# Moving the low parts of the first layer's weights to GpSimd, giving taps back to VectorE, and spreading reciprocals by transposes

## The chip, the cores and the metric

The kernel runs on one core of one Trainium2 chip. The metric is the device time of one execution in microseconds; the kernel before has a median of 1711.2 us over three runs. The engines are named as the profile names them: PE is TensorE (PEld its weight loads), DVE is VectorE, ACT is ScalarE, POOL is GpSimd, SP is SyncE, which issues the DMAs.

## The reference

Two layers over 1024 tokens of width 1024, in fp32. The first is a convolution module, the second an attention with three head groups. Each is followed by `x <- LayerNorm(alpha * x + sublayer(x))`.

```python
# layer 1
a, a_gate, z = split(x @ w_in + b_in, 3)                 # 1024 -> 3 x 1024
u = a * sigmoid(a_gate)
u = causal_depthwise_conv(u, w_dw, width=31) + b_dw       # 31 taps, each channel by itself
u = silu(layer_norm(u))                                   # over the channels
y = (u * silu(z)) @ w_out + b_out
# layer 2
k, v = x @ kv_w;  q, z = x @ w_in                         # 3 groups x 16 heads x 64
for each group (window, dilation) in (128, 1), (512, 4), (2048, 16):
    o, lse = banded_attention(q, k, v, alibi)
o = sum(softmax over the groups(lse) * o)
y = (o * silu(z)) @ w_out + b_out
```

## The kernel before

**Split precision.** Every large product is made of three products of fp32r operands: high part by high part, low by high, high by low. So each weight tile of 128x1024 is loaded (`raw`), its high part is made by a copy (`whi`, line 234 on ACT in the first layer, line 236 on POOL in the second), and its low part by a subtraction, `raw - hi` (`wlo`, line 243). The set `DVE_LO` says for which weights, counted in order of use, DVE does that subtraction; for the others POOL does it. Weights 0 to 23 are those of the input projection, 24 to 39 those of the out-projection, and from 40 on those of the second layer. The first two are made in four pieces. Each of `raw`, `whi` and `wlo` has two buffers.

**First layer.** Channels lie on the partitions, in eight blocks c = 0..7, and the tokens are in two halves h of 512. PE makes the value and the gate for the eight blocks (tiles `pa`, `pg`), then the eight blocks of z (`pz`). ACT and DVE make `u` from them. The convolution of block c is called `c<n>` for the first half and `d<n>` for the second. Of its 31 taps, tap 0 is on ACT; for the next `n_pool - 1` ACT makes a product (`cvt`, line 410) and POOL adds it (line 414); the rest are on DVE, multiply and add in one instruction, into a PSUM bank (`cva`, line 426). For the twelve convolutions of `MERGED` the two sums run side by side and DVE joins them at the end (line 438); the other four, `d4` to `d7`, continue POOL's sum on DVE. `stats` then makes the mean by a product with ones on PE (`mp`, line 451), the centred values (line 465), squares on ACT, their sums on POOL and PE (`vp`), a square root and a reciprocal; `apply` makes the normalised and gated values and splits them for the out-projection (`uh` on ACT, `ul` on DVE, line 537). The out-projection (`po`) follows for each half, then the post-norm, transposes of the result (`pt`, line 730) and the split `x1h`, `x1l`.

**Second layer.** For each of eight pairs of heads PE makes k, q (`pk`, `pq`), the gate (`pzb`) and v (`pv`), scores (`ps`), transposes of the weights of attention (`ptp`, line 1156) and the products with v (`av`). The attention of one pair is done in between the projections of the next. In `finish`, the reciprocals of the softmax sums, which stand with the tokens on the partitions, are widened by ACT to a tile `rx` of 64 equal columns for each head, and PE turns them, four blocks of 128x128 for each token half, by a product with the identity into a PSUM bank (`rb`, line 1302), which DVE multiplies into the output.

**Order.** The instructions are not written out by hand. Each step is added with its engine, an estimated cost, a priority, what it waits for, and buffers it takes and frees. `Order.run` plays a list schedule with these costs and latencies on simulated engines, and the program is then emitted in that order; so the costs set only the order of each engine's instructions and of the DMA issues, which stays fixed on the chip.

```python
        @on("pe", 0.88, (2.8, a.p, 5), [widen] + a.turned[1], take="cv", frees=[widen])
        def spread():
            q.t = bank("rb", "cv")
            for j in range(4):
                nc.tensor.matmul(q.t[:, j * P:(j + 1) * P], lhsT=q.x[:, j].rearrange("p i d -> p (i d)"), rhs=ident,
                                 start=True, stop=True)
```

Of the kernel before, what the change touches and what calls it, by code (L numbers as in the profile page):

```python
# [15 lines left out]
P = 128  # L16
D = 1024
T = 1024
KT = D // P
# [8 lines left out]
PAD = 32  # L28
N_POOL = dict.fromkeys(("d4", "d5", "d6", "d7"), 12)
PE_ORDER = "a0 a1 a2 a3 a4 a5 a6 a7 z0 z1 z2 z3 z4 z5 z6 z7".split()  # L30
DVE_ORDER = "c0d0 c1c2 d1c3 c4d2 c5c6 d3c7 s0 m0 d4d5 d6d7 s1 m1".split()
FIRST = 4
X_LATE = 0.6
DVE_LO = {0, 2, 3, 8, 9, 11, 12, 14, 15, 17, 19, 20, 23, 24, 25, 26, 27, 31, 33, 34, 35, 38, 39, 41, 42, 44, 45, 46, 90, 92, 93, 94, 98, 100, 101, 102, 103, 104, 105, 106, 108, 110, 111, 112, 113, 114, 115, 117, 118, 119, 124, 125, 126, 130, 131, 133, 134, 136}
PATHS = {(0, 1): 'dp', (1, 1): 'dd', (2, 1): 'pd', (3, 1): 'pd', (0, 0): 'pd', (2, 0): 'pd', (3, 0): 'dd'}
SUMS = [8, 4]
MERGED = "c0d0c1c2d1c3c4d2c5c6d3c7"
PAIRED = (1, 2, 3, 4)
RELEASE = 0.25
ENGINES = ("pe", "act", "dve", "pool", "dma", "none")  # L40
LATENCY = {(a, b): 2.0 if a == "dma" else 0.2 if a == "pe" else 0.27 if b == "pe" else 0.08 if a == "pool" else 0.15
# [8 lines left out]
class Step:  # L50
    def __init__(self, eng, cost, fn, prio, table, take):
        self.eng, self.cost, self.fn, self.prio, self.table, self.take = eng, cost, fn, prio, table, take
        self.waits, self.then, self.users, self.frees = 0, [], 0, []


class Order:
# [4 lines left out]

    def add(self, eng, cost, fn, prio, after=(), take=None, frees=(), table=None):
        step = Step(eng, cost, fn, prio, table, take)
        for o in after:
            step.waits += 1
            o.then.append(step)
        for o in frees:
            self.free(step, o)
        self.steps.append(step)
        return step  # L70
# [5 lines left out]
    def run(self):  # L76
# [8 lines left out]
        while True:  # L85
# [28 lines left out]
            while events and events[0][0] <= now:  # L114
                _, _, _, other, step = heapq.heappop(events)
                for o in step.frees if other is None else ():
                    o.users -= 1
                    if not o.users:
                        live[o.take] -= 1
                for o in step.then:  # L120
                    if o.eng == other:
                        o.waits -= 1
                        if not o.waits:
                            heapq.heappush(heaps[other], (o.key, o))
# [6 lines left out]
def block_kernel(ctx: ExitStack, tc: tile.TileContext, x, xT, a_w_in, a_vec, a_w_out, rows,  # L131
                 w_k, w_q, w_z, w_v1, w_v23, b_w_out, cst, dist, out, dbg=None):
    nc = tc.nc
# [137 lines left out]
    def project(name, w, src, h, prio):  # L271
# [3 lines left out]
        def part(k):  # L275
            @on("pe", 0.68, prio + (k,), ([b.last] if k else []) + w.ready(k, KT) + src.steps[h][k],
                take=None if k else "pj", frees=w.slots + src.slots[h] if k == KT - 1 else [])
            def mm():
                if k == 0:
                    b.t = pj(name)  # L280
                for i, (u, v) in enumerate(((w.hi, src.hi), (w.hi, src.lo), (w.lo, src.hi))):
                    nc.tensor.matmul(b.t, lhsT=u[:, k, :], rhs=v[h][:, k, :],  # L282
                                     start=k == 0 and i == 0, stop=k == KT - 1 and i == 2)
            b.first, b.last = b.first or mm, mm
# [158 lines left out]
    def mean_of(h, y, last):  # L443
        b = mean[h]
        summed[h].append(y)

        @on("pe", 0.86, (0, 0), [last, cst_in] + ([b.last] if b.first else h * [var[0].first]), take=None if b.first else "av")
        def mm(start=b.first is None, stop=len(summed[h]) == KT):
# [61 lines left out]
    def apply(c, h, idx):  # L510
# [22 lines left out]

        @on("dve", 0.86, (0.5, c), [hi], take="hp", frees=[y.first])
        def lo():
# [5 lines left out]
    for idx, group in enumerate(DVE_ORDER):  # L541
        for i in range(0, len(group), 2):
            what, n = group[i], int(group[i + 1])
            if what in "cd":
                conv(n, int(what == "d"), N_POOL.get(group[i:i + 2], 10), group[i:i + 2] in MERGED, idx)
            elif what == "s":
# [37 lines left out]
    class Out:  # L584
# [40 lines left out]
        def part(self, ch, kp, j, w, b, start, stop, n, i, end):  # L625
            src, h = self.src, self.h
            ks = (2 * kp, 2 * kp + 1)

            @on("pe", 1.38, self.prio + (n, i), w.ready() + [s for k in ks for s in src[k, h].steps] +
                ([] if start else [b.last]), take=b.tag if start else None,  # L630
# [282 lines left out]
    def scores23(a, g, o, gate):  # L913
# [24 lines left out]
        for i in range(2):  # L938
            bias = bias_of(a, g, i)
            part(i, 0.5, 0.83, [(slice(r * P, (r + 1) * P), slice(2 * r * P, (2 * r + 1) * P),  # L940
                                 slice(2 * r * P, (2 * r + 1) * P), 0, r) for r in range(4)],
# [7 lines left out]
    def swap(made, prio):  # L949
# [3 lines left out]

        @on("pe", 0.25, prio, [made], take="cv")
        def fold_in():
# [89 lines left out]
    def vals(srcs, by_block, gate, n, end=False):  # L1045
# [26 lines left out]
        def part(t, kh, i):  # L1072
# [12 lines left out]
            def cols(x, q, kk):  # L1085
# [3 lines left out]

            @on("pe", 1.45, n + (i,), ws[kh].ready() + ready + ([b.last] if b.last else []),  # L1090
                take=None if b.first else "pj", frees=ws[kh].slots + slots)
# [55 lines left out]
    def turn(a, blocks, after, frees):  # L1147
# [3 lines left out]

        @on("pe", 0.085 * n, (2.8, a.p, 4), after + a.flip, take="cv", frees=frees)
        def flip():
# [135 lines left out]
    def finish(a, n):  # L1289
# [7 lines left out]

        @on("pe", 0.88, (2.8, a.p, 5), [widen] + a.turned[1], take="cv", frees=[widen])
        def spread():
            q.t = bank("rb", "cv")  # L1300
            for j in range(4):
                nc.tensor.matmul(q.t[:, j * P:(j + 1) * P], lhsT=q.x[:, j].rearrange("p i d -> p (i d)"), rhs=ident,  # L1302
                                 start=True, stop=True)

# [208 lines left out]
```

## Time and profile before

| | |
|---|---|
| median of three runs | 1711.2 us (1710.54 to 1713.39) |
| the profiled execution | 1710.37 us, span 1708.6 us, mean granted clock of PE 0.983 |
| busy in the span | PE 1637.9 us, DVE 1074.4, ACT 887.9, POOL 834.1 |
| instructions | 25230 |

The span runs from the first to the last instruction of the core; the execution's own time is 1.8 us longer. An engine is busy while an instruction of its runs, and that includes the time in which an instruction that has started is held up by something other than a semaphore.

### The profile page before, as it was taken

Reading aid. Unit: us, or ns where it says so; the run is one execution under the profiler, and the core shown is the slowest. Engines: PE = TensorE matmul, PEld = TensorE weight load, DVE = VectorE, ACT = ScalarE, POOL = GpSimd, SP = SyncE. Lnnn points to the kernel's source line nnn. Section 1 sums busy time; section 2 is a strip of 40 time slices with the busy share of each in tenths; the row PEclk is TensorE's granted clock in tenths of the full one; section 3 lists DMA queues with packets and bytes.
Section 4 is the critical chain, followed back from the end, with each engine's and each line's share of the span. In section 5 each row is a group of like instructions: output and inputs, shape, how many; then the busy total and the mean of one; then the engine's idle time right before and its main releaser. Section 6 shows DMA issues by size and latency. Waiting matters only on the chain.

```text
span 1708.6 us, 25230 instructions
## 1 busy us (share of the span) xinstructions
PE 1637.9 (96%) x9396; PEld 1419.1 (83%) x9396; DVE 1074.4 (63%) x2293; ACT 887.9 (52%) x1986; POOL 834.1 (49%) x490
## 2 busy tenths in 40 slices
PE   8999968999899999999999999999999999999966
PEld 6888856767789988988988998898898899889855
DVE  7999999978664554554365365546536554653475
ACT  7666636265228525725743663664284275339432
POOL 5999957348333444444344435432432242233563
PEclk9999989999899999999999999999999999999988
DMA  5111111544211111101101101210120111135532
GB/s 190 50 50 41 59 37 50 174 140 155 74 38 38 38 38 62 37 29 65 45 26 48 64 26 38 66 47 25 38 75 26 38 62 38 38 103 186 193 99 86
DMA packets 43803, 116.67 MB, mean 68 GB/s; under 512 B 4512, under 2 KB 5792, under 8 KB 43680
## 3 DMA queue, kind: packets, MB, share of 16 engines
q1 hardware_dynamic: 43680, 115.06, 20.1%
q8 instruction: 74, 1.21, 0.3%
q14 instruction: 49, 0.40, 0.1%
HBM read 97.21 MB, written 17.83 MB: 67 GB/s over the span
## 4 chain that ended last, share of the span: by engine, by line
PE 69%; DVE 2%; ACT 1%; POOL 1%; DMA 1%; issue 0%; DVEq 0%; SPq 0%; POOLq 0%; ACTq 0%
PE pq L282 15%; PE pk L282 15%; PE pv L1099 15%; PE po L638 5%; PE pzb L282 5%; PE ptp L1156 4%; PE ps L866 3%; PE ps L867 3%; PE av L1175 2%; PE av L1172 2%; PE rb L1302 1%; DMA ulb<-o_d 1%; DVE x1b L1066 1%; POOL r L610 0%; DVE r L699 0%
## 5 line engine op out<-in xcount | busy, mean ns | idle before, releaser
L236 POOL TENSOR_SCALAR whi<-wraw 128x1024 fp32r<-128x1024 f32 x80 | 223.4, 2792 | 509.5 <-PE pv L1099 149.3
L243 POOL TENSOR_TENSOR wlo<-wraw,whi 128x1024 fp32r<-128x1024 f32 (+1 forms) x82 | 191.2, 2332 | 114.0 <-ACT whi L234 109.9
L414 POOL TENSOR_TENSOR y<-y,cvt 128x512 f32<-128x512 f32 x152 | 205.8, 1381 | 23.4 <-ACT cvt L410 18.6
L426 DVE SCALAR_TENSOR_TENSOR cva<-u,av,cva 128x512 f32<-128x512 f32 x308 | 209.0, 744 | 0.5
L822 DVE TENSOR_TENSOR kl<-pk,kd 64x512 fp32r<-64x512 f32 x192 | 132.2, 689 | 106.3 <-ACT kd L818 56.8
L1166 DVE TENSOR_TENSOR pl<-ptp,ph 128x384 fp32r<-128x384 f32 (+1 forms) x192 | 108.5, 587 | 105.1 <-ACT ph L1161 98.8
L870 DVE CUSTOM_DVE_ANT_0 s<-ps,bias 128x256 f32<-128x256 f32 (+1 forms) x384 | 122.6, 371 | 53.6 <-PE ps L867 53.3
L282 PE MATMUL pk<-x1h,whi 128*128 128x512 f32 x384 | 154.0, 401 | 0.0
L282 PE MATMUL pq<-x1h,whi 128*128 128x512 f32 x384 | 153.8, 401 | 0.0
L282 PE MATMUL pk<-x1h,wlo 128*128 128x512 f32 x384 | 150.6, 392 | 1.6 <-DVE wlo L243 1.6
L282 PE MATMUL pq<-x1h,wlo 128*128 128x512 f32 x384 | 150.7, 392 | 0.0
L282 PE MATMUL pq<-x1l,whi 128*128 128x512 f32 x384 | 150.5, 392 | 0.0
L282 PE MATMUL pk<-x1l,whi 128*128 128x512 f32 x384 | 150.2, 391 | 0.0
L852 ACT ACTIVATE qs<-pq 64x512 fp32r<-64x512 f32 x96 | 56.9, 593 | 174.3 <-PE pq L282 173.6
L1099 PE MATMUL pv<-whi,x1h 128*128 128x256 f32 x512 | 147.1, 287 | 0.0
L1099 PE MATMUL pv<-wlo,x1h 128*128 128x256 f32 x512 | 144.9, 283 | 0.0
L1099 PE MATMUL pv<-whi,x1l 128*128 128x256 f32 x512 | 144.9, 283 | 0.0
L410 ACT ACTIVATE cvt<-u,av 128x512 f32<-128x512 f32 x152 | 106.2, 719 | 53.9 <-POOL y L414 52.2
L818 ACT ACTIVATE kd<-pk 64x512 fp32r<-64x512 f32 x96 | 56.8, 592 | 141.7 <-PE pk L282 140.8
L1161 ACT ACTIVATE ph<-ptp 128x384 fp32r<-128x384 f32 (+1 forms) x192 | 93.0, 513 | 61.7 <-PE ptp L1156 47.2
L243 DVE TENSOR_TENSOR wlo<-wraw,whi 128x1024 fp32r<-128x1024 f32 (+1 forms) x60 | 98.9, 1649 | 32.2 <-POOL whi L236 16.9
L857 DVE TENSOR_TENSOR qs<-pq,qs 64x512 fp32r<-64x512 f32 x96 | 66.1, 688 | 77.4 <-ACT qs L852 75.1
(163 smaller groups left out, 4532.5 us busy)
## 6 DMA issues: line engine op xcount, KB each, us to landing
wraw<-in_w_k_dram SPq DMA_DIRECT2D x24, 512.0 KB, 3.4
wraw<-in_w_q_dram SPq DMA_DIRECT2D x24, 512.0 KB, 3.5
wraw<-in_w_v_dram SPq DMA_DIRECT2D x24, 512.0 KB, 3.5
wraw<-in_a_w_in_dram SPq DMA_DIRECT2D x22, 512.0 KB, 3.5
wraw<-in_a_w_out_dram SPq DMA_DIRECT2D x16, 512.0 KB, 3.5
wraw<-in_b_w_out_dram SPq DMA_DIRECT2D x16, 512.0 KB, 3.6
xraw<-in_xT_dram SPq DMA_DIRECT2D x16, 256.0 KB, 4.6
wraw<-in_w_z_dram SPq DMA_DIRECT2D x8, 512.0 KB, 3.4
```

The source lines that it names most:

```text
L236: nc.gpsimd.tensor_scalar(self.hi[:, s], self.raw[:, s], 1.0, None, op0=OP.mult)
L243: eng.tensor_sub(self.lo[:, s], self.raw[:, s], f32(self.hi[:, s]))
L282: nc.tensor.matmul(b.t, lhsT=u[:, k, :], rhs=v[h][:, k, :], start=k == 0 and i == 0, stop=k == KT - 1 and i == 2)
L410: nc.scalar.activation(q.t, src, AF.Copy, scale=wc)
L414: nc.gpsimd.tensor_add(y.t, y.t, q.t)
L426: nc.vector.scalar_tensor_tensor(y.t if s == TAPS - 1 and not merged else o.t, src, wc, y.t if s == n_pool else o.t, op0=OP.mult, op1=OP.add)
L638: nc.tensor.matmul(b.t, lhsT=u, rhs=v[:, k % 2, :], start=start and k == ks[0] and m == 0, stop=stop and k == ks[1] and m == 2)
L822: nc.vector.tensor_sub(d, src, f32(views(g, h, b, own, o.kd[i], own)[0]))
L870: nc.vector.tensor_tensor_reduce(s, ps, bias, op0=OP.add, op1=OP.max, scale=1.0, scalar=NEG, accum_out=acc)
L1099: nc.tensor.matmul(o, lhsT=cols((X1.hi, X1.lo)[u], u, kk), rhs=w[:, kk, :], start=k == 0 and m == 0 and t % 2 == 0, stop=k == KT - 1 and m ...
L1161: nc.scalar.activation(o.ph[:, :n * P], o.t[:, :n * P], AF.Copy)
L1166: nc.vector.tensor_sub(o.pl[:, :n * P], o.t[:, :n * P], f32(o.ph[:, :n * P]))
```

## The change

Four things are edited. The 23 numbers below 40 leave `DVE_LO`, so POOL makes the low parts of all first-layer weights. `n_pool` goes from 12 to 10 for `d4` to `d7` and from 10 to 9 for the other twelve convolutions, so that many fewer taps are on POOL (and their products on ACT) and as many more on DVE. In `finish` the four products with the identity become four transposes. And several estimated costs of the scheduler are changed, with a new waiting time `late` for a step, which is 0.0 for the only step that names it.

```diff
-N_POOL = dict.fromkeys(("d4", "d5", "d6", "d7"), 12)
+N_POOL = dict.fromkeys(("d4", "d5", "d6", "d7"), 10)
...
-DVE_LO = {0, 2, 3, 8, 9, 11, 12, 14, 15, 17, 19, 20, 23, 24, 25, 26, 27, 31, 33, 34, 35, 38, 39, 41, 42, 44, 45, 46, 90, 92, 93, 94, 98, 100, 101, 102, 103, 104, 105, 106, 108, 110, 111, 112, 113, 114, 115, 117, 118, 119, 124, 125, 126, 130, 131, 133, 134, 136}
+DVE_LO = {41, 42, 44, 45, 46, 90, 92, 93, 94, 98, 100, 101, 102, 103, 104, 105, 106, 108, 110, 111, 112, 113, 114, 115, 117, 118, 119, 124, 125, 126, 130, 131, 133, 134, 136}
...
+MEAN_LATE = 0.0
...
-                        if not o.waits:
+                        if not o.waits and o.late:
+                            heapq.heappush(events, (now + o.late, len(order), -2, "late", o))
+                        elif not o.waits:
                             heapq.heappush(heaps[other], (o.key, o))
...
-            @on("pe", 0.68, prio + (k,), ([b.last] if k else []) + w.ready(k, KT) + src.steps[h][k],
+            @on("pe", 0.69, prio + (k,), ([b.last] if k else []) + w.ready(k, KT) + src.steps[h][k],
...
-        @on("pe", 0.86, (0, 0), [last, cst_in] + ([b.last] if b.first else h * [var[0].first]), take=None if b.first else "av")
+        @on("pe", 0.86, (0, 0), [last, cst_in] + ([b.last] if b.first else h * [var[0].first]), take=None if b.first else "av", late=MEAN_LATE)
...
-        @on("dve", 0.86, (0.5, c), [hi], take="hp", frees=[y.first])
+        @on("dve", 1.3, (0.5, c), [hi], take="hp", frees=[y.first])
         def lo():
             g.lo = hp("ul", F32R)
...
-                conv(n, int(what == "d"), N_POOL.get(group[i:i + 2], 10), group[i:i + 2] in MERGED, idx)
+                conv(n, int(what == "d"), N_POOL.get(group[i:i + 2], 9), group[i:i + 2] in MERGED, idx)
...
-            @on("pe", 1.38, self.prio + (n, i), w.ready() + [s for k in ks for s in src[k, h].steps] +
+            @on("pe", 1.4, self.prio + (n, i), w.ready() + [s for k in ks for s in src[k, h].steps] +
...
-            part(i, 0.5, 0.83, [(slice(r * P, (r + 1) * P), slice(2 * r * P, (2 * r + 1) * P),
+            part(i, 0.87, 0.83, [(slice(r * P, (r + 1) * P), slice(2 * r * P, (2 * r + 1) * P),
...
-        @on("pe", 0.25, prio, [made], take="cv")
+        @on("pe", 0.15, prio, [made], take="cv")
         def fold_in():
...
-            @on("pe", 1.45, n + (i,), ws[kh].ready() + ready + ([b.last] if b.last else []),
+            @on("pe", 1.49, n + (i,), ws[kh].ready() + ready + ([b.last] if b.last else []),
...
-        @on("pe", 0.085 * n, (2.8, a.p, 4), after + a.flip, take="cv", frees=frees)
+        @on("pe", 0.092 * n, (2.8, a.p, 4), after + a.flip, take="cv", frees=frees)
...
-        @on("pe", 0.88, (2.8, a.p, 5), [widen] + a.turned[1], take="cv", frees=[widen])
+        @on("pe", 0.44, (2.8, a.p, 5), [widen] + a.turned[1], take="cv", frees=[widen])
         def spread():
             q.t = bank("rb", "cv")
             for j in range(4):
-                nc.tensor.matmul(q.t[:, j * P:(j + 1) * P], lhsT=q.x[:, j].rearrange("p i d -> p (i d)"), rhs=ident,
-                                 start=True, stop=True)
+                nc.tensor.transpose(q.t[:, j * P:(j + 1) * P], q.x[:, j].rearrange("p i d -> p (i d)"), ident)
```

## Rows read from the trace of the kernel before

**Rows 1.** The page: busy time by engine, then busy tenths in 40 equal slices.

```profile
PE 1637.9 (96%) x9396; PEld 1419.1 (83%) x9396; DVE 1074.4 (63%) x2293; ACT 887.9 (52%) x1986; POOL 834.1 (49%) x490
...
PE   8999968999899999999999999999999999999966
...
DVE  7999999978664554554365365546536554653475
...
POOL 5999957348333444444344435432432242233563
```

**Rows 2.** Windows: busy us of each engine, granted clock, DMA.

```profile
0.00:436.00 436.00, 400.56 (x1676) 315.56 (x1677) 404.55 (x556) 251.57 (x365) 324.25 (x227) 0.97 0.29 96
...
232.00:262.00 30.00, 24.59 (x86) 18.40 (x87) 29.79 (x45) 8.96 (x15) 11.28 (x8) 0.84 0.21 70
262.00:300.00 38.00, 33.55 (x129) 24.58 (x128) 36.25 (x39) 25.94 (x38) 27.47 (x18) 0.96 0.12 42
470.00:1550.00 1080.00, 1073.51 (x6840) 963.61 (x6839) 566.75 (x1554) 559.36 (x1445) 432.55 (x217) 1.00 0.14 47
```

**Rows 3.** What PE waited for, 0 to 440 us: total us, times, longest.

```profile
PE pz L282 <- DVE wlo L243: 9.5, 1, 9.5
PE mp L451 <- DVE y L438: 5.4, 1, 5.4
...
PE pa L282 <- ACT whi L234: 5.3, 2, 5.0
PE mp L451 <- DVE y L426: 4.5, 1, 4.5
PE po L638 <- DVE ul L537: 2.0, 2, 1.7
```

**Rows 4.** DVE in order of time: start us, length us, instructions.

```profile
200.29 12.59 DVE L426 SCALAR_TENSOR_TENSOR cva<-u,av,cva 128x512 f32<-128x512 f32 x19
212.87 19.10 DVE L243 TENSOR_TENSOR wlo<-wraw,whi 128x1024 fp32r<-128x1024 f32 x1
...
281.60 6.90 DVE L537 TENSOR_TENSOR ul<-y,uh 128x512 fp32r<-128x512 f32 x4
...
435.04 1.22 DVE L243 TENSOR_TENSOR wlo<-wraw,whi 128x1024 fp32r<-128x1024 f32 x1
```

**Rows 5.** POOL in order of time, the run beside the long DVE operation.

```profile
204.71 26.17 POOL L414 TENSOR_TENSOR y<-y,cvt 128x512 f32<-128x512 f32 x21
```

**Rows 6.** The tile wlo, DVE to 435 us, POOL to 440 us (ns min/median/max).

```profile
L243 DVE TENSOR_TENSOR wlo<-wraw,whi x26: 417/1319/19098, 5.3 to 406.7; 128x1024 fp32r<-128x1024 f32 x22, 128x256 fp32r<-128x256 f32 x4
...
L243 POOL TENSOR_TENSOR wlo<-wraw,whi x21: 733/2403/2437, 6.1 to 416.0; 128x1024 fp32r<-128x1024 f32 x17, 128x256 fp32r<-128x256 f32 x4
...
  PEld pk L282: 0.3, 1
```

**Rows 7.** Groups by line on DVE, 0 to 436 us: busy us, mean ns.

```profile
L243 DVE TENSOR_TENSOR wlo<-wraw,whi 128x1024 fp32r<-128x1024 f32 (+1 forms) x27 | 54.6, 2023 | 6.2 <-ACT whi L234 6.2
```

**Rows 8.** The tiles cva and ul, 0 to 440 us (ns min/median/max).

```profile
L426 DVE SCALAR_TENSOR_TENSOR cva<-u,av,cva x308: 656/744/757, 22.8 to 336.1; 128x512 f32<-128x512 f32 x154
...
L537 DVE TENSOR_TENSOR ul<-y,uh x16: 676/680/1786, 281.6 to 375.8; 128x512 fp32r<-128x512 f32 x16
```

**Rows 9.** Groups by line on POOL, 0 to 436 us.

```profile
L414 POOL TENSOR_TENSOR y<-y,cvt 128x512 f32<-128x512 f32 x152 | 205.8, 1381 | 23.4 <-ACT cvt L410 18.6
```

**Rows 10.** The tile rb, whole span: the product that spreads the reciprocals.

```profile
L1302 PE MATMUL rb<-cs,rx x128: 272/275/276, 595.1 to 1612.4; 128*128 128x128 f32 x128
```

**Rows 11.** The chain that ended last, 590 to 600 us: start, us, what.

```profile
592.52 0.33 PE ptp L1156 x3
...
595.29 1.78 PE rb L1302 x16
```

**Rows 12.** The tile pz, 0 to 440 us: first and last start.

```profile
L282 PE MATMUL pz<-xh,wlo x128: 388/389/795, 188.7 to 311.1; 128*128 128x512 f32 x128
```

**Rows 13.** The chain, 0 to 440 us: the last transposes of x1.

```profile
435.27 1.09 PE pt L730 x4
```

More of the change, by code (lines that the diff above doesn't have):

```diff
@@ L50, with __init__ @@
 class Step:
-    def __init__(self, eng, cost, fn, prio, table, take):
-        self.eng, self.cost, self.fn, self.prio, self.table, self.take = eng, cost, fn, prio, table, take
+    def __init__(self, eng, cost, fn, prio, table, take, late):
+        self.eng, self.cost, self.fn, self.prio, self.table, self.take, self.late = eng, cost, fn, prio, table, take, late
         self.waits, self.then, self.users, self.frees = 0, [], 0, []
@@ L60, in __init__, with add @@
         self.bufs, self.steps = bufs, []
-    def add(self, eng, cost, fn, prio, after=(), take=None, frees=(), table=None):
-        step = Step(eng, cost, fn, prio, table, take)
+    def add(self, eng, cost, fn, prio, after=(), take=None, frees=(), table=None, late=0.0):
+        step = Step(eng, cost, fn, prio, table, take, late)
         for o in after:
@@ L115, in run @@
                 _, _, _, other, step = heapq.heappop(events)
+                if other == "late":
+                    heapq.heappush(heaps[step.eng], (step.key, step))
+                    continue
                 for o in step.frees if other is None else ():
```

## The prediction

> **What bounds the kernel now.** I read the page's slices first: TensorE is busy for 96% of the span, and its only slices with a 6 lie near 213 to 256 us and at the end [rows 1]. In the same first slices VectorE (DVE) and GpSimd (POOL) are at 9 too, which happens nowhere later. So the second layer is bound by TensorE, and in the first one three engines are nearly full at once. The windows say where it breaks: from 470 to 1550 us TensorE is busy for 1073.5 of 1080 us at full clock, so any PE time removed there is worth its full length, and no more than 6.5 us of waits are left to win; in the first 436 us it is busy for 400.6, and the clock is granted in full but for stretches such as 232 to 300 us [rows 2]. Third, the waits of PE up to 440 us: 9.5 us for one low part of a weight made on DVE, 5.4 and 4.5 us in the mean products for a convolution result of DVE, 2.0 us for DVE's low parts of the out-projection's input [rows 3]. Behind the 5.3 us for the first high part at the start, the long waits are all for DVE.
>
> Why is DVE late? Its order of time shows 19 taps in 12.59 us, 0.663 us each, and then one low part of 128x1024 that takes 19.10 us [rows 4]. The median low part takes 1.3 us [rows 6], one that meets nothing 1.22 [rows 4]. In those 19 us GpSimd runs 21 additions in 26.17 us, 1.25 us each with no gap, and DVE's operation ends when that run has ended (204.71 + 26.17 = 230.88, DVE at 231.97) [rows 4, 5]. The subtraction reads two SBUF tensors, as POOL's additions do. The taps, whose accumulator is in PSUM, never exceed 757 ns [rows 8]. So the 9.5 us wait, and the 5.4 us wait behind it, come from a subtraction that stood behind POOL's additions. The Trainium skill, "SBUF — State Buffer", Who interferes with whom, says that a DVE instruction with two SBUF inputs contends with a GpSimd instruction that reads SBUF, and that the second to issue waits until the first is done. The trace agrees on who contends; it doesn't on the size: by the page this one would have taken about 1.2 + 1.3 = 2.5 us and DVE would win 16.6 us less than I count below, but PE's own waits, which I count by, stay as they are measured.
>
> **The change, part by part.** *Low parts.* Weights 0 to 39 are the first layer's; 23 of them had their low part on DVE, weight 0 as four quarters. DVE's low parts to 436 us take 54.6 us, of which the last, of weight 41, stays (1.2): 53.4 us leave DVE, 17.9 of them the one stall [rows 4, 7]. POOL gets 22 whole ones at 2.40 us and four quarters; the quarter's minimum of 0.73 and a quarter of the whole at 0.60 bound these, 4 x 0.8 = 3.2: 56 us more on POOL [rows 6]. The high parts stay on ScalarE, no load is added, and each low part keeps its wait on the high part and its release of the raw buffer.
>
> *Taps.* d4 to d7 go from 11 to 9 POOL taps and the twelve others from 9 to 8: 8 + 12 = 20 taps. DVE gains 20 x 0.663 = 13.3 us; POOL loses 20 x 1.38 = 27.6 us [rows 4, 9]; ScalarE loses 20 products, which I cost at nothing since it is busy for only 251.6 of 436 us [rows 2] (if an addition waits for a product that cover is a gain, not a loss).
>
> *Sum over the first layer.* DVE: 404.6 - 53.4 + 13.3 = 364.5 us. POOL: 324.3 + 56 - 27.6 = 352.7 us [rows 2]. DVE falls by 40 us, more than PE can use: what PE can win is its own waits, 9.5 + 5.4 + 4.5 + 2.0 = 21.4 us [rows 3], and the half clock behind them, (1 - 0.84) x 30 + (1 - 0.96) x 38 = 6.3 us by the windows of 232 to 300 us [rows 2]; together 27.7 us, the upper bound. Something comes back on DVE, since POOL is fuller: the low parts of the out-projection's input take 0.68 us by the median and 1.79 at the longest [rows 8], and four of them in a row 6.90 us, 1.7 each, while POOL was busy [rows 4]. The median says that about half go unhindered, those of the second token half; now these 8 and the 4 products with the gate that DVE does beside them can meet POOL: 12 x 1.05 = 12.6 us at worst, nothing at best. I take a third, 4.2 us, for only those that PE is waiting for count. The first layer ends 23.5 us earlier, between 15 (all 12.6 given back) and 27.7.
>
> What is late next, when the stall goes? DVE's convolutions end earlier by the stall's 17.9 us at least, and the statistics and the out-projection's input with them; behind DVE stands POOL, with 353 us of work in the 412 that are left, 86% against 74%. A low part on POOL waits in POOL's one queue behind at most the additions that the order puts ahead, and it stands ahead of the taps by priority. The layer has 17 whole POOL low parts now, and no matmul waited for one: the only wait charged to them is 0.3 us of a weight load [rows 6], while the longest wait of PE for a low part is charged to DVE [rows 3].
>
> *Reciprocals.* For each pair of heads 8 products of 128x128 in fp32 become 8 transposes. The products are 128 instructions over eight pairs, two for each [rows 10], and the chain passes through all 16 of a pair, 1.78 us; three transposes of the same size take 0.33 us of it, 0.11 each [rows 11]. So 8 x 0.11 = 0.88 us replace 1.78: 0.90 us a pair, 7.2 us over eight. Seven of the eight lie in the stretch where PE is full, so they count in full; the eighth is worth between 0 and 0.9. Bounds: nothing, if a transpose costs two instructions as well, to 7.2. I take 7.2. The trace shows the granted clock at 1.00 across all 470 to 1550 us, with 78 other transposes a pair inside [rows 2]. The Trainium skill, "TensorE: Matmul & The Clock Gate", Part 4, says that a transpose doesn't count as activity for the clock, which speaks against this part; by it the clock could drop around the eight places, and the saving would be gone. The trace doesn't bear it out at this length of work.
>
> *The order.* The scheduler's costs change (first-layer matmuls 0.68 to 0.69, split of the low part 0.86 to 1.3, the reduction of scores 0.5 to 0.87, and others), so every engine's static order may shift, and the DMA issues with it. No row prices that. Where PE is full, it can win the 6.5 us left there [rows 2] and lose a like amount by new waits; I take 0. The waiting time 'late' is 0 and does nothing.
>
> **The sum** is made against the profiled execution's 1710.4 us (span 1708.6, 1.8 around it), 0.8 under the median of 1711.2: 1710.4 - 23.5 - 7.2 = 1679.7, so 1680.
>
> **The rivals.** *GpSimd becomes the bound behind 230 us.* About 12 of the moved low parts lie there, each 2.40 - 1.2 = 1.2 us slower [rows 6]; if PE waits for every one, 14.4 us come back: 1694. Standing behind one addition each time adds 12 x 1.38 = 16.6: 1711 at worst. For it: POOL at 86%. Against it: no matmul waited for POOL's low parts so far.
>
> *The block of DVE by POOL comes back (slower than before).* POOL now runs longer unbroken stretches, and DVE still has multiplications and subtractions with two SBUF inputs behind the statistics. One such block costs 17.9 us [rows 4]; it needs two on the path, 35.8 us, to outweigh 30.7: 1716, and decides from 34 us on. For it: one in the run before, which nothing in the program order forbids again. Against it: the four low parts at 281 us met POOL and took turns with it, 1.7 us each [rows 4].
>
> *The transposes give nothing* (two instructions each, or the clock): 1687.
>
> *All of it comes*, and the new order wins in layer two as well: 1710.4 - 27.7 - 7.2 - 6.5 = 1669.
>
> **How the numbers follow.** A time within 0.2%, 3.4 us, can't be told from no change here. Forecast 1680 (own range 1672 to 1692) 0.62; GpSimd the bound, around 1694, 0.16, a quarter of it beyond 1699; transposes give nothing 0.08; below 1669, 0.04; the block again, slower, 0.07; the parts cancel near 1710, 0.03. The range 1669 to 1699 leaves out 0.04 + 0.04 + 0.07 + 0.03 = 0.18. Faster: 0.62 + 0.15 + 0.08 + 0.04 = 0.89; same: 0.03 + 0.01 = 0.04; slower 0.07.
>
> **What would show it.** The profile after should have no DVE low part above 3 us in the first 300 us, no PE wait for one before the second layer, full clock up to the end of the gate projections, and those ended some 15 to 25 us before the 311 of now [rows 12]; the mean products' waits gone or under 2 us; POOL's L243 group to 436 us at about 100 us and the additions x132; the first layer's end (the last transposes of x1) near 412 instead of 436 [rows 13]; the group of the spread products x64 at half the time. I am wrong if PE waits for POOL's low parts or for DVE's low parts of the out-projection's input, or if the second layer's own stretch changes by more than 7 us.

## The result and the profile after

The changed kernel takes 1693.5 us in the median of four executions (1690.65 to 1695.26). The kernel before, run beside it four times, takes 1712.3 us. The ratio is 0.9889 (95% interval 0.987 to 0.9907): 18.8 us or 1.1% faster. The time lies in the range given, 1669 to 1699, but 13.5 us above the forecast of 1680 and just outside that forecast's own range of 1672 to 1692. The profiled execution of the changed kernel took 1695.3 us (span 1693.5), 15.1 less than that of before.

One thing has to be known for what follows. Executions of the kernel before fall into two groups some 17 us apart. Of 91 that ran beside the experiments, 58 lie near 1694 us and 33 near 1711, and nothing lies between 1697 and 1709. The four that ran beside the result were all of the upper group, and so is the execution shown ahead of the prediction. The ratio above and its interval thus compare with the upper group alone.

The page of the changed kernel, against [rows 1]:

```profile
PE 1630.9 (96%) x9332; PEld 1410.2 (83%) x9332; DVE 1047.0 (62%) x2287; ACT 872.4 (52%) x1966; POOL 852.6 (50%) x496
...
PE   7999999988999999999999999999999999999976
...
DVE  7999999896663653654364365446536654653475
...
POOL 6989995678233444355344444432433242232553
```

TensorE's (PE's) 6 near 213 to 256 us is gone; the first slice is at 7 instead of 8, and the two near 339 to 423 us are at 8. VectorE (DVE) falls to 6 one slice earlier, and GpSimd's (POOL's) dip to 5 is one slice later. The windows of the same kernel, with the columns of [rows 2]:

```profile
0.00:436.00 436.00, 413.79 (x1745) 326.89 (x1746) 383.02 (x574) 239.93 (x350) 343.48 (x234) 0.98 0.29 97
470.00:1550.00 1080.00, 1070.31 (x6856) 960.68 (x6855) 565.59 (x1537) 571.07 (x1506) 428.05 (x216) 1.00 0.15 48
```

The granted clock stays at 1.00 over 470 to 1550 us. What PE waited for up to 440 us, against [rows 3]:

```profile
PE pt L736 <- DVE x1l L752: 6.8, 7, 2.3
PE pa L288 <- ACT whi L240: 5.4, 2, 4.9
PE pa L288 <- POOL wlo L249: 3.5, 1, 3.5
PE po L644 <- POOL wlo L249: 2.0, 2, 1.8
PE mp L457 <- DVE y L432: 2.0, 1, 2.0
PE pk L288 <- POOL wlo L249: 1.0, 1, 1.0
```

The waits of 9.5, 5.4 and 4.5 us are gone, and 2.0 is left at a mean product. New are 6.5 us for low parts made on POOL. The 6.8 us for DVE's x1l are an old wait grown by 1.4; the prediction's sum left it out, though it is longer than two of the four that it counted. In the kernel before:

```profile
PE pt L730 <- DVE x1l L746: 5.4, 3, 2.9
```

POOL by line up to 436 us, against [rows 6, 9]:

```profile
L420 POOL TENSOR_TENSOR y<-y,cvt 128x512 f32<-128x512 f32 x132 | 170.2, 1312 | 14.1 <-ACT cvt L416 10.8
L249 POOL TENSOR_TENSOR wlo<-wraw,whi 128x1024 fp32r<-128x1024 f32 x39 | 94.9, 2436 | 47.3 <-ACT whi L240 30.8 <-DMA row<-in_rows_dram 10.1 <-DMA r<-in_x_dram 3.6
```

Where the time went shows in the stages. Each line is the start or end of one tile's instructions in the two profiled executions:

| stage | before, us | after, us | difference |
|---|---|---|---|
| convolution gates (pg) ended | 187.6 | 193.9 | +6.3 |
| DVE centres the first half | 249.5 | 225.6 | -23.9 |
| gate projections (pz) ended | 311.5 | 296.6 | -14.9 |
| DVE centres the second half | 339.9 | 318.2 | -21.7 |
| out-projection, second half, began | 364.4 | 348.8 | -15.6 |
| out-projection ended | 418.1 | 404.7 | -13.4 |
| first layer ended (last pt) | 436.4 | 424.4 | -12.0 |

So 6.3 us are lost by 194 us, 21.9 are won from there to 349 us, and 3.6 are lost again to the layer's end. The second layer's stretch, up to the last spread (tile `rb`), became 5.6 us shorter, and the end behind it 2.5 longer: -12.0 - 5.6 + 2.5 = -15.1.

The loss at the start, in PE's order of time and in POOL's:

```profile
29.64 0.40 PE L288 MATMUL pa<-xl,whi 128*128 128x512 f32 x1
33.55 0.79 PE L288 MATMUL pa<-xh,wlo 128*128 128x512 f32 x1 [3.52 <-POOL wlo L249]
34.14 0.63 PE L288 MATMUL pa<-xh,whi 128*128 128x512 f32 x1
```

```profile
28.56 2.63 POOL L420 TENSOR_TENSOR y<-y,cvt 128x512 f32<-128x512 f32 x2
31.15 4.68 POOL L249 TENSOR_TENSOR wlo<-wraw,whi 128x1024 fp32r<-128x1024 f32 x2
```

And the window behind the wait, with the columns of [rows 2]:

```profile
33.50:40.00 6.50, 6.45 (x16) 5.09 (x17) 6.50 (x11) 1.74 (x3) 6.42 (x5) 0.53 0.47 161
```

PE waits 3.52 us for the low part of weight 2, which stands behind two additions in POOL's queue. Then its products take 0.63 instead of 0.40 us: the granted clock is 0.53 from 33.5 to 40 us, near the lower level of 1.2 GHz, and 1.00 before 29.5 and behind 40. (1 - 0.53) x 6.5 = 3.1 us; with the 3.5 that is the 6.3, within 0.3. A second profile of the same kernel, shown with the experiments, has a shorter wait here and no half clock, so part of this loss is one execution's.

The transposes, as tile and in the chain, against [rows 10, 11]:

```profile
L1308 PE MATMUL rb<-cs,rx x64: 270/273/274, 578.6 to 1594.8; 128*128 128x128 f32 x64
```

```profile
578.74 0.87 PE rb L1308 x8
```

### The profile page after: what moved, and what is told of

It reads as the page before. It is cut to its first block, busy times and chain, and to the rows that moved or that the text cites. A ratio compares the mean times of both kernels' runs of the same rounds, so it can differ in the third digit from the quotient of the medians.

```text
span 1693.5 us, 25050 instructions
## 1 busy us (share of the span) xinstructions
PE 1630.9 (96%) x9332; PEld 1410.2 (83%) x9332; DVE 1047.0 (62%) x2287; ACT 872.4 (52%) x1966; POOL 852.6 (50%) x496
## 4 chain that ended last, share of the span: by engine, by line
PE 85%; DVE 6%; ACT 3%; POOL 2%; DMA 2%; issue 1%; SPq 0%; DVEq 0%; POOLq 0%; ACTq 0%
PE pk L288 15%; PE pv L1105 15%; PE pq L288 14%; PE po L644 9%; PE pzb L288 5%; PE pa L288 5%; PE pg L288 5%; PE ptp L1162 4%; PE ps L872 3%; PE ps L873 3%; PE pz L288 3%; PE av L1181 2%; PE av L1178 2%; DVE cva L432 2%; DMA ulb<-o_d 1%
## 5 line engine op out<-in xcount | busy, mean ns | idle before, releaser
L249 POOL TENSOR_TENSOR wlo<-wraw,whi 128x1024 fp32r<-128x1024 f32 (+1 forms) x108 | 249.1, 2309 | 120.8 <-ACT whi L240 100.1
L432 DVE SCALAR_TENSOR_TENSOR cva<-u,av,cva 128x512 f32<-128x512 f32 x328 | 222.4, 747 | 0.9
L420 POOL TENSOR_TENSOR y<-y,cvt 128x512 f32<-128x512 f32 x132 | 170.2, 1312 | 14.1 <-ACT cvt L416 10.8
L1172 DVE TENSOR_TENSOR pl<-ptp,ph 128x384 fp32r<-128x384 f32 (+1 forms) x192 | 109.3, 588 | 102.5 <-ACT ph L1167 97.8
L416 ACT ACTIVATE cvt<-u,av 128x512 f32<-128x512 f32 x132 | 91.0, 717 | 44.3 <-POOL y L420 43.6
L1021 ACT ACTIVATE s<-s,nm 128x128 f32<-128x128 f32 (+1 forms) x256 | 113.8, 464 | 0.0
```

The source lines that it names most:

```text
L249: eng.tensor_sub(self.lo[:, s], self.raw[:, s], f32(self.hi[:, s]))
L420: nc.gpsimd.tensor_add(y.t, y.t, q.t)
L432: nc.vector.scalar_tensor_tensor(y.t if s == TAPS - 1 and not merged else o.t, src, wc, y.t if s == n_pool else o.t, op0=OP.mult, op1=OP.add)
L1021: nc.scalar.activation(s, s, AF.Exp, scale=SCALE, bias=a.nm2[:, 2 * i + n, r:r + 1], accum_out=a.d23[:, g - 1, i, n, r:r + 1])
L1172: nc.vector.tensor_sub(o.pl[:, :n * P], o.t[:, :n * P], f32(o.ph[:, :n * P]))
```

## The experiments

My theory after the result: the 19.10 us subtraction of DVE [rows 4] is a block by POOL's run of additions, and the change wins by having no low part on DVE that can be blocked. There are two rivals: the change wins by moving work off a full DVE, block or no block; or the start's loss can be undone and the forecast reached. Low parts and taps were tried apart and together, and then the block by itself. "Lower" and "upper" are the two groups of before in the same set of runs. There are four sets, on three chips; their lower medians are 1694.2, 1693.8, 1694.8 and 1694.1, the upper ones 1711.3, 1712.0, 1711.6 and 1710.4.

**Only the transposes**, in before (this edit is called T below):

```diff
-                nc.tensor.matmul(q.t[:, j * P:(j + 1) * P], lhsT=q.x[:, j].rearrange("p i d -> p (i d)"), rhs=ident,
-                                 start=True, stop=True)
+                nc.tensor.transpose(q.t[:, j * P:(j + 1) * P], q.x[:, j].rearrange("p i d -> p (i d)"), ident)
```

> The kernel before with one edit: the products that spread the reciprocals are transposes; order and all else as before. Theory (two instructions become one, each on the path of a full TensorE): 64 instead of 128 instructions in that group and 6.3 to 7.2 us less, about 1704.5 against 1711. Rival (a transpose costs as much as an fp32 product, or lowers the clock): within 1 us of before.

Six executions lie at 1690.4 (1689.9 to 1691.9) and four at 1707.0 (1706.0 to 1707.5): 3.8 and 4.3 us under before's two groups, with the ratio of all at 0.9983 (0.9935 to 1.003). The chain shows the pair's price, and the waits of PE behind 440 us show where a part goes:

```profile
596.34 0.87 PE rb L1302 x8
```

```profile
PE po L638 <- ACT uhb L1318: 8.5, 1, 8.5
```

A pair takes 0.87 instead of 1.78 us, as forecast. The final projection waits 8.5 us for its input instead of 7.6, so 0.9 us comes back there. Of the 7.2 forecast about 4 are left.

**Weights 2 and 3 back on DVE**, in the changed kernel:

```diff
-DVE_LO = {41, 42, 44, ..., 136}
+DVE_LO = {2, 3, 41, 42, 44, ..., 136}
```

> The changed kernel with the low parts of weights 2 and 3 back on DVE. Theory (in the changed kernel TensorE stood for 3.5 us at 30 us for weight 2's low part, which stood on GpSimd behind two additions, and restarted at half clock): that wait gone, the gate projections of the eight blocks end at 188 instead of 194 us, and the kernel is 4 to 6.5 us faster than the changed one, about 1688. Rival (the start is given back, since DVE and GpSimd are the bound after 220 us): less than 1.5 us faster, 1692 or more.

Median 1699.0 (1696.2 to 1702.7), ratio 1.0012 (0.9985 to 1.0039). The start was mended (pg ended at 188.8, pz at 290.4) and the time was lost behind it. The waits of PE up to 440 us:

```profile
PE po L644 <- DVE r L662: 5.9, 1, 5.9
...
PE pt L736 <- POOL r L709: 5.1, 6, 1.6
```

The second half of the out-projection ran from 341.7 to 407.1, 65.4 us instead of 55.9, and the first layer ended at 424.6, as in the changed kernel. What the start gives is lost to DVE and POOL at the layer's end. The 3.7 us by which this profile is longer still lie behind the first layer: the granted clock over 424 to 470 us is 0.95, where the changed kernel has 1.00, which is 2.3 us, and the rest is open. "The start can be mended" falls.

**Only weight 19's low part to POOL**, in before. This is the blocked one:

```diff
-DVE_LO = {0, ..., 17, 19, 20, ..., 136}
+DVE_LO = {0, ..., 17, 20, ..., 136}
```

> The kernel before with one edit: the low part of weight 19, the one that took 19.1 us on DVE, is made on GpSimd. Theory (one block behind a run of additions makes most of what was won in the first layer): no DVE low part above 3 us, first layer 12 to 18 us shorter, about 1696. Rival 1 (the total load of DVE in the first layer is what counts, 40 us less in the change): only the 1.2 us of one low part, within 3 us of before. Rival 2 (another low part is blocked instead): a long one elsewhere, within 3 us of before.

All ten executions form one group, 1701.4 (1699.4 to 1703.7): 7.2 over the lower group and 9.9 under the upper. DVE's and POOL's order of time:

```profile
224.65 7.96 DVE L243 TENSOR_TENSOR wlo<-wraw,whi 128x1024 fp32r<-128x1024 f32 x1
```

```profile
216.56 14.95 POOL L414 TENSOR_TENSOR y<-y,cvt 128x512 f32<-128x512 f32 x12
```

The block did not go; it moved to the next low part of DVE, weight 20's, and again ended with POOL's run (216.56 + 14.95 = 231.51, DVE at 232.61). 7.96 less the usual 1.3 is 6.7 us, which is about the 7.2.

**The costs as before**, in the changed kernel, all but the 0.44 of the spread:

```diff
-            @on("pe", 0.69, prio + (k,), ...
+            @on("pe", 0.68, prio + (k,), ...
...
-        @on("dve", 1.3, (0.5, c), [hi], take="hp", frees=[y.first])
+        @on("dve", 0.86, (0.5, c), [hi], take="hp", frees=[y.first])
...
```

> The changed kernel with the scheduler's costs of the kernel before, but for the transposes' 0.44; the low parts, the taps and the transposes are as changed. Theory (the costs only shuffle orders): within 3 us of the changed kernel. Rival (the new costs carry part of the gain by a better order, above all the 1.3 of the out-projection input's low part and the 0.87 of the scores): 4 us or more slower than the changed kernel, with more waits of TensorE for DVE.

Median 1695.3 (1693.6 to 1697.7), ratio 0.9982 (0.9952 to 1.0013). The order that the new costs make is worth 2 to 3 us against the changed kernel's 1692.4 to 1693.5.

**Both kernels again, unedited**, to see the groups:

> The kernel before, unedited, profiled again and timed against itself. Theory (the 19.1 us operation is an accident of an execution, not of the program: the times of before in the first four runs of experiments fall into two groups, 1692 to 1697 and 1710 to 1714): both groups again, a quarter to a half of the executions in the upper one; a profile from the lower group shows weight 19's low part at 1.2 to 2.5 us, no wait of TensorE of 9.5 us, and a first layer that ends 15 to 18 us before 436. Rival (the groups differ in something else, such as loads or the clock): a profile of the lower group still has a DVE low part of about 19 us.

> The changed kernel, unedited, timed beside the executions of before on one chip. Theory (it has no such operation in the first layer, since DVE makes no low part there): one group only, 1690 to 1697, so within 3 us of the lower group of before and 16 to 20 us under the upper one. Rival (it has a real gain in undisturbed executions as well): 4 us or more under the lower group of before.

Before: five executions of 1692.3 to 1696.8 and five of 1709.7 to 1712.8. After: one group, 1690.3 to 1696.1, median 1692.4, ratio 0.9947 (0.9907 to 0.9986). So the change is worth 19.6 us against the upper group and 1.4 against the lower.

The execution of after that was profiled here (span 1688.5) differs from the first one at the start. First its wait of PE, then the window behind it with the columns of [rows 2]:

```profile
PE pa L288 <- POOL wlo L249: 1.9, 1, 1.9
```

```profile
33.50:40.00 6.50, 6.50 (x31) 5.33 (x30) 6.50 (x11) 2.20 (x4) 6.42 (x5) 1.00 0.47 161
```

PE stood for 1.9 us instead of 3.5, and the clock stayed at 1.00 instead of 0.53. The convolution gates ended at 190.5, the second half of the out-projection began at 342.6, and the first layer ended at 419.7, 16.7 us before that of the kernel before and not 12.0.

**Only the low parts**, in before:

```diff
-DVE_LO = {0, 2, 3, 8, ..., 38, 39, 41, 42, ..., 136}
+DVE_LO = {41, 42, ..., 136}
```

> The kernel before with one edit: the low parts of weights 0 to 39 all on GpSimd; taps, products and costs as before. Theory (GpSimd, with 27.6 us of additions more than in the change, becomes the bound, and the low parts stand behind them): one group of times, no long DVE operation, 5 to 12 us above the lower group of before, about 1699 to 1706, with TensorE waiting for GpSimd's low parts. Rival (GpSimd has room enough): within 3 us of the lower group of before.

Median 1734.7 (1733.0 to 1735.4), ratio 1.0176 (1.0087 to 1.0265): 41 us over the lower group. First the waits of PE, then the windows with the columns of [rows 2], then DVE's order of time:

```profile
PE mp L451 <- DVE y L426: 27.1, 3, 24.3
```

```profile
300.00:340.00 40.00, 38.31 (x161) 30.07 (x160) 11.89 (x18) 9.44 (x11) 36.22 (x23) 0.99 0.34 116
340.00:380.00 40.00, 11.18 (x15) 3.79 (x14) 36.82 (x66) 11.04 (x19) 6.98 (x5) 0.57 0.23 81
```

```profile
336.80 1.95 DVE L426 SCALAR_TENSOR_TENSOR cva<-u,av,y 128x512 f32<-128x512 f32 x1
```

From 300 to 340 us GpSimd is busy for 36.2 of 40 us and DVE for 11.9; from 340 us PE stands for DVE's taps, and the clock is 0.57. DVE itself stood before the tap at 336.80. The profile charges 16.7 us of that to a part of the out-projection on PE, which ended at 336.15 and whose reader is ahead of the tap in DVE's queue. POOL's additions, which the tap continues, ended at 335.83, so the two came within 0.4 us of each other. That GpSimd is the bound is argued from its load and from that coincidence; no wait here shows it.

**Weight 19 back on DVE**, in the changed kernel:

```diff
-DVE_LO = {41, 42, 44, ..., 136}
+DVE_LO = {19, 41, 42, 44, ..., 136}
```

> The changed kernel with the low part of weight 19 alone put back on DVE. Theory (the block needs only a DVE subtraction with both inputs in SBUF that starts inside a run of additions on GpSimd): a second group of executions comes back, 10 to 20 us above the first, or the profile shows that operation above 3 us. Rival (the block belongs to the exact order of the kernel before, where 21 additions run without a gap): one group, within 3 us of the changed kernel.

One group, 1694.8 (1691.4 to 1696.2). In DVE's order of time, and in POOL's:

```profile
216.31 1.39 DVE L249 TENSOR_TENSOR wlo<-wraw,whi 128x1024 fp32r<-128x1024 f32 x1 [1.03 <-ACT whi L240]
```

```profile
207.79 21.98 POOL L420 TENSOR_TENSOR y<-y,cvt 128x512 f32<-128x512 f32 x16
```

The same subtraction began in the middle of a run of 16 additions and took 1.39 us. A long run alone does not make a block.

**Before once more**, one execution, in the hope of a profile without the block:

> The kernel before, unedited, one more profile, to see an execution of the lower group (1692 to 1697). Theory (the block alone makes the difference of the groups): if the time is below 1700, weight 19's low part takes 1.2 to 2.5 us, TensorE does not wait 9.5 us for it, and everything behind it up to the last transposes of the first layer is 15 to 18 us earlier. Rival: a time below 1700 with an operation of 19 us in the profile. A time above 1705 would show the operation a fourth time and leave this open.

It took 1709.7 us and had the block (19.15 us, ended 1.09 after POOL's run). No execution of the lower group was profiled. All six profiles of kernels whose times fall in two groups are of the upper one, though of before's executions only a third are; whether that is chance, or profiling favours the block, is open.

**Only the taps**, in before:

```diff
-N_POOL = dict.fromkeys(("d4", "d5", "d6", "d7"), 12)
+N_POOL = dict.fromkeys(("d4", "d5", "d6", "d7"), 10)
...
-                conv(n, int(what == "d"), N_POOL.get(group[i:i + 2], 10), group[i:i + 2] in MERGED, idx)
+                conv(n, int(what == "d"), N_POOL.get(group[i:i + 2], 9), group[i:i + 2] in MERGED, idx)
```

> The kernel before with one edit: 20 taps move from GpSimd to DVE; low parts, products and costs as before. Theory (in the first layer DVE is the engine that TensorE waits for, so 13.3 us more on it lengthen the layer, and the taps pay only beside the low parts): 5 to 13 us above the lower group of before, about 1700 to 1707, with longer waits for DVE. Rival (GpSimd was the bound and its relief of 27.6 us wins): 3 us or more below the lower group. The block may come in some executions.

Four executions lie at 1697.4 to 1699.1, one at 1703.1, five at 1710.6 to 1713.6; ratio 1.0029 (0.9986 to 1.0072). Against the lower group it costs 3 to 4 us. The profiled one had a block of 12.46 us at weight 19's low part, which ended at 228.46 with POOL's run (207.35 + 20.04 = 227.39).

**Transposes, and weight 18 on DVE in the place of 19**, in before with T:

```diff
-DVE_LO = {0, ..., 17, 19, 20, ..., 136}
+DVE_LO = {0, ..., 17, 18, 20, ..., 136}
```

> The kernel before with the transposes, and with the low parts of weights 18 and 19 exchanged between DVE and GpSimd (DVE makes 18, GpSimd 19), so that both engines keep their loads. Theory (the block belongs to weight 19's place in the run of additions): one group, 1688 to 1693, so 1 to 4 us below the changed kernel. Rival (any low part on DVE near that run can be blocked): a second group of 1705 to 1710 again. Rival 2 (the order is shuffled against it): one group at 1696 to 1702, as with weight 19 alone moved.

Three executions at 1690.5 to 1691.3, seven at 1703.0 to 1707.0; ratio 0.9993 (0.9946 to 1.004). DVE's order of time, then POOL's:

```profile
223.32 13.85 DVE L426 SCALAR_TENSOR_TENSOR cva<-u,av,y 128x512 f32<-128x512 f32 x1
```

```profile
217.89 18.72 POOL L414 TENSOR_TENSOR y<-y,cvt 128x512 f32<-128x512 f32 x15
```

This time no low part is blocked, but a tap: the one whose second tensor is y, in SBUF, where the other taps have their accumulator in PSUM. It too ended with the run (236.61, DVE at 237.17).

**A pause in POOL's runs**, in before with T. Behind 68 of its 152 additions POOL writes zeros into a tile of 128x1 that nothing reads; no low part and no tap moves:

```diff
+    pause = consts.tile([P, 1], F32, name="pause")
...
+                if s % 2 == 0:
+                    nc.gpsimd.memset(pause, 0.0)
```

> The kernel before with the transposes, in the same order as that experiment, and with a clearing of one unused column (128x1) on GpSimd after every second of its convolution additions: 68 small instructions of about 0.1 us, which read nothing and change no result. Theory (a DVE instruction with both inputs in SBUF waits until GpSimd's run of additions has a break, and a break without reads lets it in): no DVE operation above 4 us in the profile, and one group of times at 1689 to 1696, where the same kernel without the clearings has a second group at 1706 to 1708. Rival (such a short instruction is no break; the operation waits until GpSimd's queue has run dry): an operation of 15 to 20 us again in the profile, and two groups 16 us apart.

Twelve executions form one group, 1689.5 (1688.1 to 1691.1), ratio 0.9937 (0.9904 to 0.997), the best of all kernels here. DVE's order of time, then POOL's, then the last transposes of x1 as tile, and last a wait of PE:

```profile
213.11 1.87 DVE L244 TENSOR_TENSOR wlo<-wraw,whi 128x1024 fp32r<-128x1024 f32 x1
```

```profile
210.10 3.79 POOL L415 TENSOR_TENSOR y<-y,cvt 128x512 f32<-128x512 f32 x3
213.84 0.09 POOL L417 MEMSET pause<- 128x1 f32 x1
213.90 2.24 POOL L415 TENSOR_TENSOR y<-y,cvt 128x512 f32<-128x512 f32 x1
```

```profile
L733 PE MATMUL pt<-cs,r x32: 272/374/447, 405.4 to 417.8; 128*128 128x128 f32 x32
```

```profile
PE mp L454 <- DVE y L429: 4.5, 1, 4.5
```

Weight 19's low part, which took 19.10 us in [rows 4] and 19.04 in the profile of the transposes alone, takes 1.87. It ended at 214.98, 1.09 us after the run of three additions that the memset cut off (210.10 + 3.79 = 213.89), just as the long ones ended 1.09 us after theirs; the addition that follows stretches to 2.24. Against the profiled execution with T alone, which had the block, the first layer ends 19.2 us earlier (last transpose begun at 417.8 against 437.0) and the whole is 19.4 us shorter (1688.1 against 1707.5). PE's waits of 9.5 and 5.4 us are gone from its list; the 4.5 of [rows 3] is still there.

## Why the prediction was right, and where it was not

**The stall: mechanism right, its standing wrong.** The prediction read the 19.10 us subtraction as a block by POOL's additions. The pause shows that: the same subtraction at the same place takes 1.87 us once POOL's run is broken, and the upper group is gone in 12 executions of 12. The step that failed is the first term of the sum: it took PE's waits of 9.5 and 5.4 us, and half clock behind them, as the program's own, to be won in every execution. By the times, only 33 of 91 executions have them; that those of the lower group have not is inferred from the pause, since none was profiled. In the prediction's terms the block is 9.5 + 5.4 + 4.8 us (the clock over 232 to 262 us), 19.7 of the 27.7, close to the 19.2 that the pause took off the first layer. The other 8.0 (waits of 4.5 and 2.0, the clock over 262 to 300 us) are what was there to win in every execution, and they stay in the pause kernel. Of these the changed kernel turned 4.5 into 2.0, and 2.0 into as long a wait for POOL's low parts. By the two groups of before the block of 19 us costs about 17, and that of 7.96 us in the third experiment costs 7. Against the lower group the change is worth 1.4 us. That the result reads 18.8 is owed to the draw: all four executions of before were of the upper group.

**The first layer: 23.5 forecast, 12.0 and 16.7 measured** in the two profiles of the changed kernel. Between the end of the convolution gates and the second half of the out-projection the change won 21.9 us in the first and 24.7 in the second, of the 27.7 that the sum counted before anything came back. Two costs were not in the sum. At the start 6.3 us (2.9 in the second): PE waits for weight 2's low part behind two additions, and in the first profile then runs at half clock. The prediction held against this that PE had hardly waited for POOL's low parts before; but those that PE needs first had been on DVE. At the end 3.6 us (5.1 in the second): PE's waits there are 2.0 us for low parts on POOL, which are new, and those for x1l on DVE. The 4.2 us set aside for what comes back thus became 9.9 and 8.0, at other places: the low parts of the out-projection's input, for which it was meant, took 16.8 us on DVE against 16.7 before and caused no wait of PE that its list of waits shows.

**The other 1.4 us, taken apart.** From the lower group: transposes alone 1694.2 to 1690.4, -3.8. The changed kernel with the old costs is at 1695.3, so low parts and taps together cost 4.9. The new costs give 2 to 3 back, for the changed kernel is at 1692.4 and 1693.5. The medians of the lower group in the four sets agree within 1.0 us, which is what such sums across sets can tell. Low parts and taps thus buy freedom from a block that a third of the executions have, and with the old costs they pay 4.9 us for it in every one.

**The transposes: 7.2 forecast, about 4 measured.** The local term was right, 1.78 to 0.87 us a pair. The prediction let seven of eight pairs count in full; the final projection's wait for its input grew by 0.9, and the list of waits behind 440 us has two new ones of 0.5 and 0.4. The clock behind the final projection's wait also comes back later. The second 4 us from the first product on, before, with the transposes alone, and after, with the columns of [rows 2]:

```profile
1634.50:1638.50 4.00, 4.00 (x19) 3.27 (x18) 3.37 (x5) 0.93 (x1) 0.00 (x0) 1.00 0.00 0
1630.70:1634.70 4.00, 4.00 (x17) 3.19 (x16) 2.83 (x5) 0.33 (x1) 0.00 (x0) 0.85 0.00 0
1617.80:1621.80 4.00, 4.00 (x15) 3.17 (x14) 2.38 (x4) 0.00 (x0) 0.00 (x0) 0.73 0.00 0
```

With the transposes alone that is (1 - 0.85) x 4 = 0.6 us, so 7.2 becomes 4.8, which is near the 3.8 and 4.3 of the groups, given that their medians agree within 1.0. The changed kernel's own loss of 2.5 us behind the second layer holds the same 0.9 and (1 - 0.73) x 4 = 1.1 of the clock; the last 0.5 stays open. The rule of the Trainium skill, "TensorE: Matmul & The Clock Gate", Part 4, that was weighed against this part, cost nothing that the trace shows: the clock is 1.00 over 470 to 1550 us with 86 transposes a pair.

**The costs, taken at 0,** are worth 2 to 3 us.

**The rivals.** "GpSimd becomes the bound" gave 1694, and the time is 1693.5, but by luck and not for its reason: behind 230 us PE waited for POOL's low parts 3.0 us, not 14.4. Without the taps the low parts cost 41 us. The 27.6 us that the taps take from POOL are thus what makes the change possible at all, though alone they cost 3 to 4. "The block comes back" shows in none of the times of the changed kernel, 14 executions, nor in its two profiles; four taps that read y are still there that could meet it, the longest 2.84 us in both.

**What would show it.** Seen: no DVE low part above 3 us, pz 14.9 and 21.1 us earlier in the two profiles (15 to 25 were named), the additions x132, the low parts on POOL at 102.5 us with their quarters, the spread x64 at half its time. (The quarters were priced at 0.8 us, above both figures that the prediction names as their bounds; on POOL they took 0.96.) Missed: the layer's end (424.4 and 419.7, not 412), the clock (half behind 33 us in the first profile), and the sentence that PE would not wait for POOL's low parts.

## What to carry to other kernels

A wait in one profile is one execution's. Before a 10 us wait enters a sum in full, ask whether the operation that it stands for, here one of 22 low parts that was fourteen times its siblings' length, could as well not have happened, and run the kernel before ten times more. The same goes for the kernel after, whose wait at the start is 3.5 us in one profile and 1.9 in the other. Where two engines' long runs collide, breaking the run with a 0.1 us instruction cost less than moving 23 low parts to the other engine, and won more.

## What the runs showed of the hardware

A DVE operation with two tensors in SBUF can be held for as long as POOL's unbroken run of additions lasts: 19.10 us past some 15 additions of a run of 21, 7.96, 12.46 and 13.85 us in other runs. Each ended 0.56 to 1.10 us after POOL's run ended, which is less than its own length. It hit subtractions of 128x1024 and a tap of 128x512 with y in SBUF; no tap with its accumulator in PSUM took more than 0.76 us. With a POOL instruction of 0.09 us that reads nothing in its runs, no such subtraction or tap of the first layer took more than 2.39 us. The Trainium skill, "SBUF — State Buffer", Who interferes with whom, has the second instruction wait for the first; on who contends the runs agree, on how long they do not.

Why a run of additions blocks in some executions, and lets DVE in after one addition in others (1.39 us in the middle of 16), is open; by its times the same program does both. There is no profile of before without the block; the pause kernel stands in for it.
